# Seven-product up projections of a decoder trunk: combinations of the activations in four pinned portions, sums kept in the other block's buffer, added weight blocks loaded ahead of the down projections

## The chip, the cores and the metric

One core of one Trainium2 chip. The metric is device time in microseconds (us) of one execution of the whole program, which is one launch. The engines are named as the profile names them: PE (TensorE matmul), DVE (VectorE), ACT (ScalarE), POOL (GpSimd) and SP (SyncE, which here only issues transfers). A line such as L94 is line 94 of the kernel.

## The reference

Two layers of a decoder trunk on one sequence of 512 positions with 1024 features, in float32. Per layer:

```python
h = modulate(x, norm_ffn1, sh1, sc1)
x = x + 0.5 * (1 + g1) * swiglu(h, w1, w3, w2)       # FFN 1
h = modulate(x, norm_mix, sh2, sc2)
x = x + (1 + g2) * token_mix(h, ...)                 # gated delta rule and latent attention
h = modulate(x, norm_ffn2, sh3, sc3)
x = x + 0.5 * (1 + g3) * swiglu(h, w1, w3, w2)       # FFN 2

def swiglu(h, w1, w3, w2):
    return (jax.nn.silu(h @ w1) * (h @ w3)) @ w2     # d_ff = 2816
def modulate(x, gain, shift, scale):                 # shift, scale, gate = silu(c) @ ada_w + ada_b
    return rms_norm(x, gain) * (1 + scale) + shift
```

The change touches the FFNs, and the adaLN products that are worked off beside them.

## The kernel before, in words

**Layout and precision.** x and h lie feature-major, [128, 8 k-tiles, 512 positions]. Every product is made in three passes of split operands: a value is the sum of a rounded high part and a low part, and `mm3` adds hi·hi, hi·lo and lo·hi. A weight slab of 512 KB (128x1024) is loaded into a buffer "raw", its high half is a cast on ACT (L121) and its low half a subtraction on DVE (L122).

**One FFN.** d_ff is 22 tiles of 128. The first 4 ("plain"; 6 in layer 0's first FFN, whose first tiles are worked in `begin`) are made by `up`: slabs of w1 and w3, 48 matmuls of 128x512, then a Silu on ACT and a product with the second accumulator on DVE (L514), and a split of the result. The other tiles go two at a time through `pairs`. It makes a 2x2 block product out of seven smaller ones (a Strassen–Winograd form), each 24 matmuls of 128x256. The seven weight forms are, in order, a11, f1, f2, a12, f3, f4 and a22: f1 and f3 are sums of two blocks, made by a load from SP and a second, accumulating load from POOL into the same "L" buffer (`block_sum`, L559); f2 = a11 + f1 (L588) and f4 = a12 + f2 (L591) are made on DVE; each form is then cast (ACT, L581) and gets its low half (DVE, L582). The seven combinations of h are made once per FFN by `fast_acts`, from eight quarters of h in float32, into two buffers "A". The products land in accumulators acc, sc, sm of PSUM; after each product `pairs` copies or adds them (L650 to L672), and Silu and products follow. At step 4 ACT copies the accumulator (L668) and POOL adds the copy (L669).

**The down projection** comes in three parts (`THIRDS`, 8, 8 and 6 tiles of d_ff), worked when 10, 18 and 22 tiles are up, and each adds into x (L407). In the last part, `close` makes the last four of eight tiles in halves, from "spare" slabs whose high and low parts lie in the A buffers and whose raw home is L, and works the next norm in between.

**What sets the order.** Engines run their queues in order. A scheduler sets each queue's order ahead of time, save for what `order` pins. SP issues loads in order and waits at each until its buffer is free: 2 raw, 5 L, 3 each of the split slabs. `self.queue` holds adaLN work: one block is a load of 512 KB into L and one multiply-and-reduce on DVE (L269). `tick(n)` pops n of it, in `up`, after each pair and in the down projections; `drain` pops the rest after the FFN. `rope_tables`, a chain of small DVE and ACT instructions, stands at the end of layer 0's queue.

**The beginning.** `begin` (list `BEGIN`) makes h one k-tile at a time (L1499, ACT's high part L1502, DVE's low part L1467) and adds each to seven slabs' products. The quarters come from POOL, which adds high and low part back together (L462); the first combinations (L471 to L482) are worked right behind it, before the first gate products.

## Time and profile before

| | |
|---|---|
| three runs | 2773.82, 2780.12 (median), 2790.0 us |
| the profiled execution | 2779.66 us |
| its span | 2777.9 us |
| mean granted PE clock | 0.995 |
| busy share PE, DVE, ACT, POOL | 97%, 73%, 47%, 12% |
| HBM read | 376.55 MB |
| chain that ended last, by engine | PE 73%, DVE 15%, DMA 5%, ACT 3%, issue 2%, POOL 2% |

The median of the runs lies 0.46 us above the profiled execution. In a timeline, a row has its start, its duration, engine, line, operation, the tiles by name, shapes and, in brackets, how long the engine stood idle before it and who released it. Rows of several instructions have a count behind x. In the windows the columns are the busy times of PE, PEld (weight loads), DVE, ACT and POOL with their counts, the granted clock, the DMA share and GB/s.

### The profile page before, as it was taken

The page shows a single profiled execution, that of the slowest core. Times are in us where ns is not written, and L with a number is a line of the kernel's source. Part 1 is how long each engine was busy: PE and PEld are TensorE (multiplying, and loading weights), DVE is VectorE, ACT ScalarE, POOL GpSimd, SP SyncE. Part 2 cuts the span into 40 slices and gives each one's busy share as a digit, 9 for nine tenths or more (in the row PEclk, how much of TensorE's full clock was granted, in tenths as well). Part 3 has the DMA queues.
Part 4 walks back from the last instruction along what each step waited for, and adds up shares of the span by engine and source line. Part 5 has one row for each costly group of instructions (what it writes and reads, how often), then busy time and mean ns, then how long its engine had stood idle before and what let it go on. Part 6 is the DMA issues. An engine that isn't in the chain of part 4 may idle for free.

```text
span 2777.9 us, 44536 instructions
## 1 busy us (share of the span) xinstructions
PE 2705.7 (97%) x17168; PEld 2401.9 (86%) x17168; DVE 2023.3 (73%) x3990; ACT 1299.2 (47%) x2540; POOL 335.3 (12%) x433
## 2 busy tenths in 40 slices
PE   7899999999999999999999999999999999999999
PEld 6889897788888888999989898887888888989988
DVE  7778778867668767876678787787767686686755
ACT  3535345454446535534445353554444564353533
POOL 2001004200011011111011010150000011111100
PEclk9999999999999999999999999999999999999999
DMA  7587742322222353777427777332222223456642
GB/s 282 154 246 225 225 159 92 99 66 80 70 78 78 109 186 88 236 231 183 138 69 222 225 227 227 121 104 92 71 85 64 80 78 118 160 142 200 156 132 85
DMA packets 118870, 394.66 MB, mean 142 GB/s; under 512 B 13441, under 2 KB 16129, under 8 KB 118657
## 3 DMA queue, kind: packets, MB, share of 16 engines
q1 hardware_dynamic: 106128, 350.38, 38.2%
q0 software_dynamic: 10080, 36.70, 7.6%
q10 hardware_dynamic: 2448, 4.72, 0.4%
q8 instruction: 135, 2.21, 0.3%
q14 instruction: 79, 0.64, 0.1%
HBM read 376.55 MB, written 15.20 MB: 141 GB/s over the span
## 4 chain that ended last, share of the span: by engine, by line
PE 73%; DVE 15%; DMA 5%; ACT 3%; issue 2%; POOL 2%; SPq 0%; ACTq 0%; POOLq 0%; DVEq 0%
PE acc L94 52%; PE sc L94 14%; PE sm L94 4%; DMA raw<-in_ffn_w 3%; PE sm L99 2%; DVE L L269 2%; DVE wlo L122 2%; PE po L94 1%; DMA L<-in_ffn_w 1%; DVE wlo L582 1%; DVE cv L722 1%; DVE L L854 1%; DVE L L856 1%; DMA raw<-in_w_out 1%; ACT whi L121 0%
## 5 line engine op out<-in xcount | busy, mean ns | idle before, releaser
L94 PE MATMUL acc<-hhi,whi 128*128 128x512 f32 (+1 forms) x1368 | 506.4, 371 | 10.5 <-DVE cv L722 5.7
L121 ACT CAST whi<-raw 128x512 fp32r<-128x512 f32 (+2 forms) x554 | 320.3, 606 | 395.0 <-PE acc L94 305.8
L94 PE MATMUL acc<-hlo,whi 128*128 128x512 f32 (+1 forms) x1368 | 487.2, 356 | 1.8 <-DVE hlo L1467 0.6
L94 PE MATMUL acc<-hhi,wlo 128*128 128x512 f32 (+1 forms) x1368 | 486.7, 356 | 0.0
L94 PE MATMUL acc<-O,whi 128*128 128x512 f32 x1472 | 455.1, 390 | 0.5 <-DVE O L136 0.5
L122 DVE TENSOR_TENSOR wlo<-raw,whi 128x512 fp32r<-128x512 f32 (+2 forms) x554 | 393.8, 729 | 69.4 <-ACT whi L121 62.2
L94 PE MATMUL acc<-A,whi 128*128 128x256 f32 (+1 forms) x1808 | 348.7, 292 | 7.8 <-ACT cv L668 7.8
L94 PEld LDWEIGHTS acc<-O,whi 128*128 128x128 f32 x1472 | 275.0, 188 | 57.8 <-DVE O L136 1.7
L94 PEld LDWEIGHTS acc<-A,whi 128*128 128x128 f32 x1808 | 287.0, 192 | 14.5 <-ACT cv L668 9.4
L94 PEld LDWEIGHTS acc<-hhi,whi 128*128 128x128 f32 x1368 | 259.6, 190 | 41.9 <-issue 8.3
L94 PEld LDWEIGHTS acc<-hhi,wlo 128*128 128x128 f32 x1368 | 259.2, 189 | 38.1 <-DVE wlo L122 0.9
L94 PEld LDWEIGHTS acc<-hlo,whi 128*128 128x128 f32 x1368 | 260.4, 190 | 32.8 <-POOL hlo L392 3.0
L94 PE MATMUL acc<-O,wlo 128*128 128x512 f32 x736 | 286.6, 389 | 0.0
L94 PE MATMUL acc<-A,wlo 128*128 128x256 f32 (+1 forms) x904 | 263.6, 292 | 1.0 <-DVE wlo L582 1.0
L582 DVE TENSOR_TENSOR wlo<-raw,whi 128x1024 fp32r<-128x1024 f32 x140 | 170.6, 1221 | 93.9 <-ACT whi L581 89.3
L581 ACT CAST whi<-raw 128x1024 fp32r<-128x1024 f32 x140 | 146.4, 1046 | 191.9 <-PE acc L94 87.2
L581 ACT CAST whi<-L 128x1024 fp32r<-128x1024 f32 x105 | 109.9, 1047 | 153.8 <-DMA L<-in_ffn_w 37.5
L94 PEld LDWEIGHTS acc<-A,wlo 128*128 128x128 f32 x904 | 173.9, 192 | 3.7 <-DVE wlo L582 1.2
L407 DVE SCALAR_TENSOR_TENSOR M<-acc,gate,M 128x512 f32<-128x512 f32 (+1 forms) x112 | 77.5, 692 | 131.5 <-PE acc L94 124.3
L269 DVE SCALAR_TENSOR_TENSOR L<-L,kph 128x1024 f32<-128x1024 f32 x142 | 171.4, 1235 | 0.0
L94 PEld LDWEIGHTS acc<-O,wlo 128*128 128x128 f32 x736 | 138.2, 188 | 28.7
L559 POOL DMA_DIRECT2D L<-in_ffn_w x70 | 61.2, 875 | 729.7 <-DMA L<-in_ffn_w 257.4
(431 smaller groups left out, 5499.1 us busy)
## 6 DMA issues: line engine op xcount, KB each, us to landing
raw<-in_ffn_w SPq DMA_DIRECT2D x166, 512.0 KB, 4.6
L<-in_ada_w SPq DMA_DIRECT2D x142, 512.0 KB, 4.7
raw<-in_w_in SPq DMA_DIRECT2D x108, 512.0 KB, 3.5
L<-in_ffn_w SPq DMA_DIRECT2D x105, 512.0 KB, 4.8
L<-in_ffn_w POOLq DMA_DIRECT2D x70, 512.0 KB, 7.7
raw<-in_w_branch_a SPq DMA_DIRECT2D x16, 512.0 KB, 3.5
raw<-in_w_branch_b SPq DMA_DIRECT2D x16, 512.0 KB, 3.5
raw<-in_w_out SPq DMA_DIRECT2D x16, 512.0 KB, 3.6
```

Of the source, the lines that this page charges most:

```text
L94: i = self.nc.tensor.matmul(*a, **k)
L99: i = self.nc.tensor.transpose(*a, **k)
L121: nc.scalar.copy(hi[:, s], raw[:, s])
L122: nc.vector.tensor_sub(lo[:, s], raw[:, s], hi[:, s].bitcast(F32))
L269: self.order(self.nc.vector.scalar_tensor_tensor(raw, raw, 1.0, self.condb, ALU.mult, ALU.mult, accum_out=mod[:, o:o + 1]))
L407: self.nc.vector.scalar_tensor_tensor(self.x[:, m, a:b], ps[:, a:b], gate[:, m:m + 1], self.x[:, m, a:b], ALU.mult, ALU.add)
L559: nc.gpsimd.dma_start(t, w13[l, m2, half2].rearrange("p w k c -> p (w k c)"), accum_op=ALU.add)
L581: nc.scalar.copy(hi, t)
L582: nc.vector.tensor_sub(lo, t, hi[:].bitcast(F32))
L722: nc.vector.scalar_tensor_tensor(acc[:, s:], ps[:, :SEQ - s], w[j], acc[:, s:], ALU.mult, ALU.add)
L854: nc.vector.tensor_mul(tv, f[:, j + 1:, j:j + 1].to_broadcast([P, n, w]), x[:, j:j + 1, :w].to_broadcast([P, n, w]))
L856: nc.vector.tensor_sub(x[:, j + 1:, :w], x[:, j + 1:, :w], tv)
```

## The change

Six edits:

1. `begin` writes the quarters itself, by two more ACT instructions per k-tile; the eight POOL adds go.
2. `fast_acts` works in four portions, all of its ACT and DVE instructions pinned. The first two run inside the last two plain tiles, behind the splits of their slabs; the other two in steps 0 and 1 of the first pair.
3. f2 is formed in f1's buffer (L) rather than in a11's (raw).
4. The loads of the next pair are issued in steps 1, 2, 4, 5 and 6 of a pair rather than 2 to 6, and the next pair's forms start at step 2, not 3. `early_sums` issues f1 and f3 of the first pair behind the plain tiles, and of the pair behind a down projection, ahead of that projection.
5. At step 4 DVE adds the accumulator itself (new L670).
6. In the last down projection of an FFN, each tile works off one block (ticks (1, 1) rather than (0, 0)), and the rope tables stand at place 10 of the queue rather than at the end.

```diff
-            for j in range(2):
-                for i in range(4):
-                    hi, lo = (t[:, 2 * i:2 * i + 2, j * 256:(j + 1) * 256].bitcast(F32) for t in (self.hhi, self.hlo))
-                    nc.gpsimd.tensor_add(self.quarter(i, j), hi, lo)
...
+        ordered = self.order
...
-                nc.scalar.copy(hi, t[n])
-                nc.vector.tensor_sub(lo, t[n], hi.bitcast(F32))
+                ordered(nc.scalar.copy(hi, t[n]))
+                ordered(nc.vector.tensor_sub(lo, t[n], hi.bitcast(F32)))
...
         split(places[2], b12)
+        yield
         minus_sum(b11, b21)
...
-        def up(m):
+        def up(m, make):
             s1 = up_slab(w1, m)
             s3 = up_slab(w3, m)
+            next(make)
...
             st["f1"] = block_sum(m + 1, 0, m + 1, 1)
+            if sums_first:
+                st["f3"] = block_sum(m + 1, 0, m, 0)
             yield st
...
-            f2, f4 = st["a11"], st["a12"]
-            nc.vector.tensor_add(f2, f2, st["f1"])
+            f2, f4 = st["f1"], st["a12"]
+            nc.vector.tensor_add(f2, f2, st["a11"])
...
-                    if step in (2, 3, 4, 5, 6):
+                    if step in (1, 2, 4, 5, 6):
                         got = next(nxt, None)
-                        if step == 3 and got is not None:
+                        if step == 2 and got is not None:
                             forms.append(weights(got))
+                    if step in (0, 1):
+                        next(make, None)
...
                         product(x, f, comb[4], False)
-                        u3 = half("cv")
-                        nc.scalar.copy(u3, x)
-                        nc.gpsimd.tensor_add(p5, p5, u3)
+                        nc.vector.tensor_add(p5, p5, x)
...
+        def early_sums(m):
+            lds = loads(m, True)
+            next(lds)
+            return lds
...
-                       (0, 0) if i == 2 else (2, 1))
+                       (1, 1) if i == 2 else (2, 1))
...
-        next(make)
+        lds = early_sums(plain)
         while m < plain:
-            up(m)
+            up(m, make)
             m += 1
-            next(make, None)
-        pairs(range(plain, 10, 2), comb)
+        pairs(range(plain, 10, 2), comb, lds, make)
+        lds = early_sums(10)
         down(0)
-        pairs(range(10, 18, 2), comb)
+        pairs(range(10, 18, 2), comb, lds)
+        lds = early_sums(18)
         down(1)
-        pairs(range(18, FT, 2), comb)
+        pairs(range(18, FT, 2), comb, lds)
...
             ordered(nc.scalar.activation(acts[k][0], h, AF.Identity, bias=sh))
+            for i, (a, b) in enumerate(HALVES):
+                q = self.quarters.get((k // 2, i)) or self.quarter(k // 2, i, 4)
+                ordered(nc.scalar.activation(q[:, k % 2, :], h[:, a:b], AF.Identity, bias=sh))
...
-                self.queue.append(self.rope_tables)
+                self.queue.insert(10, self.rope_tables)
```

The first place is DVE's queue at the end of the beginning, in the kernel before: the last low part (hlo), then combinations of the quarters (c, cv into A), then the low half of a slab and the first gate product.

```order
L1467 SCALAR_TENSOR_TENSOR hlo_127<-g_440,mod_77,hhi_126 128x512
L479 TENSOR_TENSOR c_88_528<-c_88_528,c_92_536 128x512
L476 SCALAR_TENSOR_TENSOR c_89_530<-c_89_530,cv_542 128x512
L472 TENSOR_TENSOR A_544<-c_88_528,A_544 128x512
L472 TENSOR_TENSOR A_544<-c_89_530,A_544 128x512
L476 SCALAR_TENSOR_TENSOR c_88_528<-c_88_528,cv_540 128x512
L476 SCALAR_TENSOR_TENSOR c_89_530<-c_89_530,c_91_534 128x512
L472 TENSOR_TENSOR A_544<-c_88_528,A_544 128x512
L476 SCALAR_TENSOR_TENSOR c_88_528<-c_88_528,c_90_532 128x512
L122 TENSOR_TENSOR wlo_473<-raw_471,whi_472 128x512 x2
L514 TENSOR_TENSOR g_479<-g_479,sc_213 128x512
```

The same place in the changed kernel, whose L511 is the gate product:

```order
L1474 SCALAR_TENSOR_TENSOR hlo_127<-g_462,mod_77,hhi_126 128x512
L122 TENSOR_TENSOR wlo_497<-raw_495,whi_496 128x512 x2
L511 TENSOR_TENSOR g_503<-g_503,sc_223 128x512
L511 TENSOR_TENSOR g_509<-g_509,sc_255 128x512
L511 TENSOR_TENSOR g_515<-g_515,sm_285 128x512
```

The eight rows of combinations stand further back now, behind the slabs of the last two plain tiles.

The second place is SP's queue in a pair between two down projections of layer 0's first FFN. Before, the next pair's loads are f1, f3 and a22 (L), then a11 and a12 (raw), then two adaLN blocks:

```order
L554 DMA L_1866<-in_ffn_w 128x1024
L554 DMA L_1934<-in_ffn_w 128x1024
L554 DMA L_2006<-in_ffn_w 128x1024
L554 DMA raw_1900<-in_ffn_w 128x1024
L554 DMA raw_1968<-in_ffn_w 128x1024
L267 DMA L_2042<-in_ada_w 128x1024
L267 DMA L_2045<-in_ada_w 128x1024
```

In the changed kernel the same pair's loads are these, with a11 first:

```order
L552 DMA raw_1892<-in_ffn_w 128x1024
L552 DMA L_1858<-in_ffn_w 128x1024
L552 DMA L_1957<-in_ffn_w 128x1024
L552 DMA L_2027<-in_ffn_w 128x1024
L267 DMA L_2063<-in_ada_w 128x1024
L552 DMA raw_1989<-in_ffn_w 128x1024
L267 DMA L_2066<-in_ada_w 128x1024
```

a11 stands ahead of the three loads into L, and an adaLN block ahead of a12.

The third place is the end of layer 0's first FFN, its last down projection. On SP before, the four spare slabs (into L) and the first slabs of the stage (raw) stand together:

```order
L118 DMA L_3452<-in_ffn_w 128x768
L118 DMA raw_3329<-in_ffn_w 128x768
L118 DMA L_3458<-in_ffn_w 128x768
L118 DMA raw_3359<-in_ffn_w 128x768
L118 DMA L_3464<-in_ffn_w 128x768
L118 DMA L_3470<-in_ffn_w 128x768
L267 DMA L_3798<-in_ada_w 128x1024
```

In the changed kernel the spare slabs (L_3477 to L_3495) come behind the stage's slabs and the blocks of its ticks (L_3440, L_3474):

```order
L267 DMA L_3440<-in_ada_w 128x1024
L118 DMA raw_3409<-in_ffn_w 128x768
L118 DMA raw_3443<-in_ffn_w 128x768
L118 DMA raw_3501<-in_w_in 128x1024
L267 DMA L_3474<-in_ada_w 128x1024
L118 DMA L_3477<-in_ffn_w 128x768
L1271 DMA spill<-M_63 128x512
L118 DMA L_3483<-in_ffn_w 128x768
L118 DMA raw_3509<-in_w_in 128x1024
L118 DMA raw_3517<-in_w_in 128x1024
L1271 DMA spill<-M_63 128x512
L118 DMA L_3489<-in_ffn_w 128x768
```

On DVE of the changed kernel, the multiply of the last block, the last spare slab's low half and two slabs of the mix stand ahead of the row that empties the first half's accumulator:

```order
L269 SCALAR_TENSOR_TENSOR L_3474,mod_77<-L_3474,kph_64 128x1024
L122 TENSOR_TENSOR A_3341<-L_3495,A_3341 128x512
L122 TENSOR_TENSOR A_3341<-L_3495,A_3341 128x256
L122 TENSOR_TENSOR wlo_3511<-raw_3509,whi_3510 128x512
L122 TENSOR_TENSOR wlo_3519<-raw_3517,whi_3518 128x512 x2
L407 SCALAR_TENSOR_TENSOR M_63<-acc_3525,gate_194_1266,M_63 128x256
```

Before, the row L407 of the first half stood with no multiply and no spare slab close ahead of it.

## The prediction

> **What bounds the kernel now.** I read the page first: the share of each engine, then the chain that ended last.

> ```profile
> PE 2705.7 (97%) x17168; PEld 2401.9 (86%) x17168; DVE 2023.3 (73%) x3990; ACT 1299.2 (47%) x2540; POOL 335.3 (12%) x433
> ```

> TensorE (PE) is busy for 97% of a span of 2777.9 us, and the change leaves its matmuls alone. So a gain can only come out of stretches in which PE waits or runs below its own pace. What I need is a list of those, with the releaser of each. The view of waits, PE alone, gives it (engine and line, who released it, us in total, times, longest).

> ```profile
> PE acc L94 <- ACT cv L668: 7.8, 8, 2.4
> PE sc L94 <- DVE g L514: 7.4, 1, 7.4
> PE sc L94 <- DVE wlo L582: 7.4, 5, 2.8
> ...
> PE acc L94 <- DVE wlo L582: 1.0, 1, 1.0
> ```

> Three rows lie in the seven-product pairs (L668 is the copy at step 4, L582 the low half of a weight form): 7.8 + 7.4 + 1.0 = 16.2 us. One row, L514, is a single wait where the first gate product is made after the kernel's beginning. These four rows bear on the change. Around the single wait, PE's timeline has this:

> ```profile
> 76.07 0.79 PE L94 MATMUL sc<-hhi,whi 128*128 128x512 f32 x1 [7.36 <-DVE g L514]
> ...
> 82.11 0.39 PE L94 MATMUL sc<-hhi,wlo 128*128 128x512 f32 x1
> 82.33 0.39 PE L94 MATMUL sc<-hhi,whi 128*128 128x512 f32 x1
> ...
> 83.95 0.39 PE L94 MATMUL sc<-hlo,whi 128*128 128x512 f32 x1
> ```

> From 82.33 to 83.95 lie seven steps, 0.23 us each. From 76.07 to 82.33, 15 matmuls took 6.26 us instead of 15 x 0.23 = 3.45. So the wait of 7.36 us drew 2.8 us of slow matmuls behind it. The windows show why, in the column behind POOL's busy time, which is the granted clock:

> ```profile
> 68.50:84.60 16.10, 8.74 (x26) 6.80 (x26) 13.17 (x20) 11.31 (x20) 2.40 (x2) 0.68 0.49 125
> ```

> It is 0.68 here. The place is worth 7.4 + 2.8 = 10.2 us.

> **The beginning: -10.2 us.** Who keeps L514 late? VectorE's (DVE) timeline:

> ```profile
> 61.96 0.75 DVE L1467 SCALAR_TENSOR_TENSOR hlo<-g,mod,hhi 128x512 fp32r<-128x512 f32 x1 [0.79 <-ACT hhi L1502]
> 65.35 1.76 DVE L479 TENSOR_TENSOR c<-c,c 128x512 f32<-128x512 f32 x1 [2.64 <-POOL c L462]
> ...
> 73.72 1.28 DVE L122 TENSOR_TENSOR wlo<-raw,whi 128x512 fp32r<-128x512 f32 x2
> 75.33 1.28 DVE L514 TENSOR_TENSOR g<-g,sc 128x512 f32<-128x512 f32 x2 [0.33 <-ACT g L513]
> ```

> Between the last low part (62) and the slab's (73.72) stand eight instructions of the combinations, the first waiting 2.64 us for GpSimd's (POOL) quarter add. ScalarE (ACT) stands in the same queue; it can neither load its table nor make the first Silu before the combinations are split:

> ```profile
> 61.20 0.73 ACT L1502 ACTIVATE hhi<-g,mod 128x512 fp32r<-128x512 f32 x1 [3.22 <-DVE mod L1500]
> ...
> 72.26 1.13 ACT L121 CAST whi<-raw 128x512 fp32r<-128x512 f32 x2
> 73.41 1.28 ACT L513 ACT_TABLE_LOAD   x1
> 74.70 1.57 ACT L513 ACTIVATE g<-acc 128x512 f32<-128x512 f32 x3
> ```

> New on ACT are 16 instructions that write the quarters, two for each of eight k-tiles. The nearest row is an ACT of this shape with a bias, 0.5 us:

> ```profile
> 402.63 0.49 ACT L391 ACTIVATE g<-g,mod 128x256 f32<-128x256 f32 x1
> ```

> In the new order DVE goes from the last low part straight to the slab and the gate products. ACT's chain from 61.9 is then: two quarters of 0.5 each, two casts 1.13, table 1.28, first Silu about 0.6, so 65.9; DVE's product ends about 66.6. PE is busy with the last sums until 76.07 - 7.36 = 68.7, so 2 us of cover remain. The stall and its slow matmuls go. What is late next would be the slab, but its casts at 72.26 wait for no transfer. The combinations move behind the slab splits of the last two plain tiles, two portions of some 5 to 7 DVE rows each, beside 11 us of matmuls per plain tile (48 x 0.23).

> Of the 16 ACTs only the two ahead of the first slab casts delay PE's first matmul (+1.0); the others lie in ACT's idle time (3.22 us in the row at 61.20). Against this stand the eight POOL adds that go, the last of them these:

> ```profile
> 62.79 2.53 POOL L462 TENSOR_TENSOR c<-hhi,hlo 128x512 f32<-128x512 f32 x2 [6.19 <-DVE hlo L1467]
> ```

> They let DVE wait, but PE is the bound of the beginning. I take 0, between -1 and +1.

> **The pairs: -16.2 us, and +6.7 of new waits.** A pair is seven products of 24 matmuls, each like this one on the chain that ended last, so 7 x 2.88 = 20.16 us:

> ```profile
> 205.18 2.88 PE acc L94 x24
> ```

> The waits on L668 come from a late transfer, as SP's queue of issues and ACT's timeline show:

> ```profile
> 236.01 6.76 SPq L554 DMA_DIRECT2D L<-in_ffn_w  x3
> 243.61 2.72 SPq L554 DMA_DIRECT2D raw<-in_ffn_w  x2
> ```

> ```profile
> 250.87 1.05 ACT L581 CAST whi<-raw 128x1024 fp32r<-128x1024 f32 x1 [3.85 <-DMA raw<-in_ffn_w]
> 251.82 0.58 ACT L668 COPY cv<-acc 128x512 f32<-128x512 f32 x1
> ```

> The next pair's first form (a11, into raw) is loaded behind three loads into L, which take SP 6.76 us of issue, and the copy that frees the accumulator stands behind its cast. The change loads a11 ahead of them, since f2 no longer keeps its buffer, and drops L668 and POOL's add (L669): DVE adds from the accumulator itself. Its price is that of the PSUM add next door:

> ```profile
> 233.83 0.68 DVE L672 TENSOR_TENSOR g<-g,sc 128x512 f32<-128x512 f32 x1
> ```

> That is +0.7 us of DVE per pair. DVE has room for it in the fullest pair that I found, 17.27 of 20.30:

> ```profile
> 1585.70:1606.00 20.30, 20.18 (x168) 20.18 (x168) 17.27 (x23) 10.76 (x17) 3.54 (x3) 1.00 0.72 237
> ```

> Behind each down projection the first f1 came late too, and held the chain on DVE:

> ```profile
> 191.09 1.23 DVE L588 TENSOR_TENSOR raw<-raw,L 128x1024 f32<-128x1024 f32 x1 [7.04 <-DMA L<-in_ffn_w]
> ```

> There the sums now are loaded a whole down projection ahead. So all 16.2 us go. What is late next is a loop through one L buffer. f1's buffer is now held until f4's sum, and the next f1 goes into the buffer that the pair's first adaLN block frees. The loop's durations, from the transfers around 205 to 270 and around 1575 to 1640 and from DVE's and ACT's rows there:

> ```profile
> L<-in_ffn_w SPq DMA_DIRECT2D x6, 512.0 KB, 5.3
> ...
> L<-in_ffn_w POOLq DMA_DIRECT2D x4, 512.0 KB, 7.9
> ```
> ```profile
> L<-in_ada_w SPq DMA_DIRECT2D x7, 512.0 KB, 9.2
> raw<-in_ffn_w SPq DMA_DIRECT2D x6, 512.0 KB, 8.1
> L<-in_ffn_w POOLq DMA_DIRECT2D x6, 512.0 KB, 8.3
> L<-in_ffn_w SPq DMA_DIRECT2D x6, 512.0 KB, 5.8
> ```
> ```profile
> 219.49 1.22 DVE L269 SCALAR_TENSOR_TENSOR L<-L,kph 128x1024 f32<-128x1024 f32 x1
> ...
> 222.91 1.22 DVE L582 TENSOR_TENSOR wlo<-L,whi 128x1024 fp32r<-128x1024 f32 x1
> ```

> Load 5.3, accumulating load 7.9, cast 1.05, low part 1.2, f2's sum 1.2, f2's cast 1.05 and low part 1.2, two small DVE rows about 0.9 (L672's 0.68 and one of half its size or less), the adaLN multiply 1.2: 21.0 us against 20.16, so 0.8 late per pair in layer 0, and 21.9 (5.8 and 8.3), 1.7 late, in layer 1. It counts only where two pairs with adaLN work stand in a row after the slack of the early loads is used: the last two of four pairs, and the third behind four plain tiles. Those are 2 pairs in layer 0's first FFN (1.6) and 3 in layer 1's (5.1); the second FFNs have too few adaLN blocks for it. I take 6.7, between 0 and 16.2 (as much as went). Net -9.5.

> [...]

> **Work moved out of the boundaries: -6.1 us.** The rope tables and four adaLN blocks are drained between layer 0's first FFN and its mix. The same 2424 matmuls run in layer 1's window without rope and with two blocks:

> ```profile
> 390.48:767.09 376.61, 369.67 (x2424) 316.20 (x2424) 278.79 (x686) 177.20 (x384) 55.61 (x85) 1.00 0.24 78
> 1765.98:2136.98 371.00, 366.43 (x2424) 314.83 (x2424) 274.70 (x670) 173.57 (x379) 56.81 (x85) 1.00 0.24 79
> ```

> The difference is 5.6 us, and I take all of it (between 3 and 6.5): one drained block instead of four, and the tables go into the first down projection. Layer 1 loses its two drained blocks, 0.5 (0 to 2.4, two of 1.2).

> **Layer 0's last down projection: +2.9 us.** The ticks that now run there put four adaLN loads on SP and in L ahead of the spare slabs. Before, these were issued from this row on, ahead of the stage, and no wait of PE names them:

> ```profile
> 353.15 0.33 SPq L118 DMA_DIRECT2D L<-in_ffn_w  x1
> ```

> Now the fourth spare slab waits for the block of the fourth tick. The stage has four tiles of 18 matmuls (18 x 0.23 = 4.1 us each, 16.5) and then halves of 18 x 0.12 = 2.2 (2.88 / 24 each); the fourth half is due 23 us in. The block's multiply stands about 17 us in, the load takes 5, casts and low parts some 2.5 (1.13 and 1.28 for 1024 columns above), and behind them on DVE stand two more slab rows (1.28) and the L407 that frees an accumulator: near 26. I take +2.9, between 0 and +6. Layer 1's queue is short enough for the spares to come first.

> **The sum.** -10.2 + 0 - 9.5 - 6.1 + 2.9 = -22.9. The profiled execution took 2779.66 us (span 2777.9), the median of the three runs is 2780.12, so I subtract from either: about 2757 us. With the best ends (-11.2, -16.2, -8.9, 0) it is -36.3 and 2743 to 2744; with the poorest (-9.2, 0, -3, +6) -6.2 and 2774.

> **Rivals.** (1) *The f1 loop has slack and the spare slabs come in time.* For it: over the whole run such a load takes less, by the page:

> ```profile
> L<-in_ffn_w SPq DMA_DIRECT2D x105, 512.0 KB, 4.8
> ```

> Against it: the crowded stretches are these pairs. It gives -22.9 - 6.7 - 2.9 = -32.5, 2747. Chance 0.17. [...]

> (2) *The other side: the L buffers become the bound of every pair with adaLN work.* Early sums hold two of five L buffers, f1 a third for longer, and adaLN blocks wait for what is left. For it: raw loads of 8.1 and adaLN loads of 9.2 in the layer 1 window, so a loop with 8.1 instead of 5.8 takes 24.2; against it: loads of L itself stay at 5.8. Over the 22 such pairs (8, 3, 9 and 2 in the four FFNs) the middle, 23.0, costs (23.0 - 20.16) x 22 = 62, less the 6.7 counted: 2757 + 55 = 2812. It makes the kernel slower by 0.5% from (22.9 + 13.9 + 6.7) / 22 = 2.0 us late, a loop of 22.1 in every such pair. Chance 0.05. (3) *The gap at the beginning is half refilled*, by the quarters on ACT or by slab transfers that now queue behind f1 and f3 on SP. Against it: 2 us of cover on ACT. It gives back some 9 of the 10.2 where the wait is again long enough for the clock to fall: 2766. Chance 0.10. (4) *The change doesn't do what it says in the pairs and at the boundary*: the waits only change their name, since the same transfers and the same DVE work stay in the same stretches. It gives -10.2 + 2.9, so 2772. Chance 0.10. My own forecast has the remaining 0.58.

> **How the numbers follow.** The predicted time is 2757, the likeliest case. The range, 2742 to 2772, takes in rival 1, rival 3, nearly all of my own case's bounds and half of rival 4; outside are rival 2 and the tails. About 0.5% (13.9 us) is what a measurement of this kernel can tell from no change. Faster than 2766.2: 0.54 of my 0.58, rival 1's 0.17, half of rival 3 (0.05), a little of rival 4 (0.03), 0.79. Slower than 2794: 0.04. The rest, 0.17, is within.

> **What would show it.** Right: PE has no wait of over 1 us on the first gate product, and the granted clock around 68 to 85 is 1.00; the waits on the step 4 accumulator are gone; PE's waits in the pairs are on the low part of f1 or f2, released by a transfer into L, in the third and fourth pair between down projections and mainly in layer 1; 2 to 4 us of waits late in layer 0's last down projection, behind spare slabs; the mix window of layer 0 is 371 long. Wrong: waits on f1 or f2 in every pair with adaLN work (rival 2), a new PE wait of several us before 85 (rival 3), or a mix window still at 376 (rival 4).

## The result and the profile after

| | before | after |
|---|---|---|
| runs | 2773.82 to 2790.0 us (4) | 2735.41 to 2742.08 us (4) |
| median | 2783.39 us | 2738.93 us |
| profiled execution, span | 2779.66, 2777.9 us | 2742.08, 2740.3 us |

The ratio is 0.9843, with a 95% interval of 0.9809 to 0.9876. Run again beside two experiments, the changed kernel gave 0.9864 (0.9841 to 0.9886). So it is faster by 1.4 to 1.6%; the two intervals together reach from 1.1 to 1.9%. The forecast of 2757 had the sign, but 2738.9 lies below its range (2742 to 2772). Profile against profile the gain is 37.6 us, and the sum had 22.9.

The page's first row after the change, and PE's waits:

```profile
PE 2695.0 (98%) x17168; PEld 2396.7 (87%) x17168; DVE 2006.5 (73%) x4025; ACT 1285.4 (47%) x2519; POOL 266.9 (10%) x390
```
```profile
PE acc L94 <- ACT O L135: 2.2, 1, 2.2
PE acc L94 <- DVE M L407: 2.2, 1, 2.2
...
PE acc L94 <- ACT g L653: 0.5, 2, 0.3
```

The four rows on which the prediction stood (16.2 us in the pairs, 7.4 at the first gate product) are gone. New are 2.2 us on L407, 2.2 us on L135, and 0.5 us in the pairs; the wait of 1.5 us on a slab's cast at 27 us (L1483, now L1490) has grown to 2.3. PE's busy time also fell by 10.7 us, although its instructions are the same 17168: some of the busy time before was slow matmuls (5.96 us of it at a clock of 0.50 from 324.31 to 331.14 us, for one).

**Where the time came from.** Both traces have the same matmuls in the same order but for fewer than a hundred, so the start of the n-th in one less that in the other shows where a gain is made. The beginning and the matmuls right behind it gave 11.1 us, the pairs 22.0, the start of layer 0's mix 6.1. The last down projection of layer 0's first FFN took 3.6 back. That of its second FFN took 4.8, of which 3.2 came back in the plain tiles behind it, where the kernel before had waits on a slab (L121, 1.1 us, and L122, 0.5) and slow matmuls of its own (a clock of 0.50 from 1433.64 to 1437.06 us). The rest, some 3.5, lies in places of at most 1.7.

At the beginning DVE now goes from the last low part (L1474) to the slab and the gate product:

```profile
57.95 0.75 DVE L1474 SCALAR_TENSOR_TENSOR hlo<-g,mod,hhi 128x512 fp32r<-128x512 f32 x1 [0.80 <-ACT hhi L1509]
64.48 1.29 DVE L122 TENSOR_TENSOR wlo<-raw,whi 128x512 fp32r<-128x512 f32 x2 [5.79 <-ACT whi L121]
66.91 1.28 DVE L511 TENSOR_TENSOR g<-g,sc 128x512 f32<-128x512 f32 x2 [1.14 <-ACT g L510]
```

The window behind it is clean, at a granted clock of 1.00 where it was 0.68:

```profile
68.00:85.00 17.00, 17.00 (x77) 14.08 (x76) 16.21 (x24) 10.48 (x19) 2.92 (x2) 1.00 0.43 138
```

The longest pair before was the first behind layer 0's second down projection. Its first matmul, its wait and the first matmul of the next pair are these:

```profile
319.13 0.28 PE L94 MATMUL acc<-hhi,whi 128*128 128x256 f32 x1
...
325.18 0.58 PE L94 MATMUL sc<-A,wlo 128*128 128x256 f32 x1 [2.78 <-DVE wlo L582]
...
344.92 0.28 PE L94 MATMUL acc<-hhi,whi 128*128 128x256 f32 x1
```

The same pair after the change:

```profile
303.62 0.28 PE L94 MATMUL acc<-hhi,whi 128*128 128x256 f32 x1
...
323.78 0.28 PE L94 MATMUL acc<-hhi,whi 128*128 128x256 f32 x1
```

It took 25.79 us with a wait of 2.78, and takes 20.16. The other 2.8 us were slow matmuls: the clock over this pair was 0.87, and it is 1.00 now. I call what a pair takes beyond 20.04 us, first to last matmul, its excess. Over all 35 pairs it was 23.9 us and is 1.9.

In layer 0's last down projection the row that empties the accumulator does stand behind slab rows on DVE, and PE waits for it, with slow matmuls behind (18 in 3.77 us instead of 2.16):

```profile
367.37 1.89 DVE L122 TENSOR_TENSOR wlo<-raw,whi 128x512 fp32r<-128x512 f32 x3
369.17 1.26 DVE L407 SCALAR_TENSOR_TENSOR M<-acc,gate,M 128x256 f32<-128x256 f32 x3
```
```profile
369.80 3.77 PE L94 MATMUL acc<-O,A 128*128 128x256 f32 x18 [2.16 <-DVE M L407]
```

### The profile page after: what moved, and what is told of

Same layout as the page of the kernel before. It is cut to its first block, busy times and chain, and to the rows that moved or that the text cites. A ratio compares the mean times of both kernels' runs of the same rounds, so it can differ in the third digit from the quotient of the medians.

```text
span 2740.3 us, 44511 instructions
## 1 busy us (share of the span) xinstructions
PE 2695.0 (98%) x17168; PEld 2396.7 (87%) x17168; DVE 2006.5 (73%) x4025; ACT 1285.4 (47%) x2519; POOL 266.9 (10%) x390
## 4 chain that ended last, share of the span: by engine, by line
PE 82%; DVE 9%; issue 3%; ACT 3%; POOL 2%; DMA 1%; SPq 0%; ACTq 0%; POOLq 0%; DVEq 0%
PE acc L94 57%; PE sc L94 16%; PE sm L94 5%; PE sm L99 2%; DVE wlo L122 2%; PE po L94 1%; DVE cv L729 1%; DVE L L861 1%; DVE L L863 1%; POOL g L821 0%; ACT whi L121 0%; POOL g L823 0%; POOL O L842 0%; DMA raw<-in_w_in 0%; ACT hhi L389 0%
## 5 line engine op out<-in xcount | busy, mean ns | idle before, releaser
L121 ACT CAST whi<-raw 128x512 fp32r<-128x512 f32 (+2 forms) x554 | 320.0, 607 | 429.2 <-PE acc L94 241.1
L94 PE MATMUL acc<-hhi,whi 128*128 128x512 f32 (+1 forms) x1368 | 506.3, 371 | 11.1 <-DVE cv L729 5.8
L94 PE MATMUL acc<-hlo,whi 128*128 128x512 f32 (+1 forms) x1368 | 487.6, 357 | 1.2 <-POOL hlo L392 0.3
L94 PE MATMUL acc<-hhi,wlo 128*128 128x512 f32 (+1 forms) x1368 | 486.7, 356 | 0.0
L122 DVE TENSOR_TENSOR wlo<-raw,whi 128x512 fp32r<-128x512 f32 (+2 forms) x554 | 387.9, 719 | 107.8 <-ACT whi L121 101.0
L94 PE MATMUL acc<-O,whi 128*128 128x512 f32 x1472 | 456.3, 391 | 2.7 <-ACT O L135 2.2
L94 PE MATMUL acc<-A,whi 128*128 128x256 f32 (+1 forms) x1808 | 346.6, 291 | 0.7 <-ACT g L653 0.5
L94 PEld LDWEIGHTS acc<-O,whi 128*128 128x128 f32 x1472 | 275.9, 188 | 60.4 <-ACT O L135 2.6
L94 PEld LDWEIGHTS acc<-hhi,whi 128*128 128x128 f32 x1368 | 259.5, 190 | 42.4 <-issue 8.3
L94 PEld LDWEIGHTS acc<-hhi,wlo 128*128 128x128 f32 x1368 | 259.4, 190 | 37.3 <-DVE wlo L1491 0.2
L94 PEld LDWEIGHTS acc<-A,whi 128*128 128x128 f32 x1808 | 286.0, 192 | 6.2 <-ACT g L653 0.9
L94 PEld LDWEIGHTS acc<-hlo,whi 128*128 128x128 f32 x1368 | 260.3, 190 | 31.7 <-POOL hlo L392 3.0
L94 PE MATMUL acc<-O,wlo 128*128 128x512 f32 x736 | 287.3, 390 | 0.0
L94 PE MATMUL acc<-A,wlo 128*128 128x256 f32 (+1 forms) x904 | 262.6, 290 | 0.0
L582 ACT CAST whi<-L 128x1024 fp32r<-128x1024 f32 x140 | 147.0, 1050 | 205.0 <-issue 77.0
L583 DVE TENSOR_TENSOR wlo<-L,whi 128x1024 fp32r<-128x1024 f32 x140 | 171.3, 1224 | 35.3 <-ACT whi L582 34.6
L94 PEld LDWEIGHTS acc<-A,wlo 128*128 128x128 f32 x904 | 173.3, 192 | 2.5
L269 DVE SCALAR_TENSOR_TENSOR L<-L,kph 128x1024 f32<-128x1024 f32 x142 | 169.9, 1220 | 5.0 <-DMA L<-in_ada_w 5.0
L583 DVE TENSOR_TENSOR wlo<-raw,whi 128x1024 fp32r<-128x1024 f32 x105 | 128.6, 1224 | 59.1 <-ACT whi L582 58.1
L582 ACT CAST whi<-raw 128x1024 fp32r<-128x1024 f32 x105 | 110.2, 1049 | 118.9 <-PE acc L94 49.3
L94 PEld LDWEIGHTS acc<-O,wlo 128*128 128x128 f32 x736 | 138.5, 188 | 28.9
## 6 DMA issues: line engine op xcount, KB each, us to landing
raw<-in_ffn_w SPq DMA_DIRECT2D x166, 512.0 KB, 4.3
L<-in_ada_w SPq DMA_DIRECT2D x142, 512.0 KB, 5.0
raw<-in_w_in SPq DMA_DIRECT2D x108, 512.0 KB, 3.4
L<-in_ffn_w SPq DMA_DIRECT2D x105, 512.0 KB, 4.5
L<-in_ffn_w POOLq DMA_DIRECT2D x70, 512.0 KB, 8.4
raw<-in_w_branch_a SPq DMA_DIRECT2D x16, 512.0 KB, 3.4
raw<-in_w_branch_b SPq DMA_DIRECT2D x16, 512.0 KB, 3.7
raw<-in_w_out SPq DMA_DIRECT2D x16, 512.0 KB, 3.5
```

Of the source, the lines that this page charges most:

```text
L94: i = self.nc.tensor.matmul(*a, **k)
L121: nc.scalar.copy(hi[:, s], raw[:, s])
L122: nc.vector.tensor_sub(lo[:, s], raw[:, s], hi[:, s].bitcast(F32))
L269: self.order(self.nc.vector.scalar_tensor_tensor(raw, raw, 1.0, self.condb, ALU.mult, ALU.mult, accum_out=mod[:, o:o + 1]))
L582: nc.scalar.copy(hi, t)
L583: nc.vector.tensor_sub(lo, t, hi[:].bitcast(F32))
```

## The experiments

All are the changed kernel with an edit undone or added. Single runs of the kernel before spread from 2769 to 2790 us, so small effects are read from the traces, place by place.

| kernel | time, us | excess of the 35 pairs, us |
|---|---|---|
| before | 2779.66 | 23.9 |
| changed | 2742.08 | 1.9 |
| changed, run again | 2740.51 | 1.2 |
| e1 quarters by POOL | 2743.87 | 4.6 |
| e2 two portions early | 2736.01 | 2.8 |
| e13 both | 2746.78 | 0.6 |
| e3 no early sums | 2740.64 | 2.3 |
| e5 f2 in a11 | 2737.22 | 0.2 |
| e4 copy and POOL's add | 2750.55 | 12.4 |
| e15 = e3 + e5 | 2749.45 | 11.5 |
| e16 = e4 + e5 | 2740.11 | 3.5 |
| e19 = e16 + old steps | 2742.56 | 2.7 |
| e20 = e19 + e3 | 2758.21 | 22.5 |
| e6 no ticks in the last down | 2737.58 | 1.6 |
| e7 rope tables at the end | 2739.60 | 0.6 |
| e8 waits of known size | 2770.34 | not read |

**The beginning: e1, e2, e13.** e1 puts the eight POOL adds back:

```diff
-                ordered(nc.scalar.activation(q[:, k % 2, :], h[:, a:b], AF.Identity, bias=sh))
...
+                    nc.gpsimd.tensor_add(self.quarter(i, j), hi, lo)
```

> The changed kernel with the quarters of layer 0's first FFN made by eight POOL adds again; the combinations stay behind the slabs of the last two plain tiles. Theory (the place of the combinations was the gap): PE has no wait of over 1 us on the first gate product, the matmuls up to the first pair end within 1 us of the changed kernel. Rival (the POOL adds were the gap): a wait of 3 to 7 us there again, and 2 to 3 us of slow matmuls behind it.

The first pair began within 0.3 us of the changed kernel's. e2 calls two portions of `fast_acts` ahead of the first gate products:

```diff
+        make = self.fast_acts(comb)
+        if begun:
+            next(make)
+            next(make)
         m = first_begun() if begun else first()
```

> The changed kernel with ACT's quarters, but the first two portions of the combinations worked ahead of the first gate products, as before. Theory (the place was the gap): a PE wait of 2 to 5 us on the first gate product, and up to 3 us of slow matmuls behind it, so 3 to 8 us lost up to the first pair. Rival (the POOL adds were the gap): no wait of over 1 us.

It lost 0.5 us. Its DVE shows why: the first combination needs no late quarter and starts ahead of the last low part (L1477).

```profile
58.50 0.68 DVE L475 TENSOR_TENSOR c<-c,c 128x512 f32<-128x512 f32 x1
59.37 0.75 DVE L1477 SCALAR_TENSOR_TENSOR hlo<-g,mod,hhi 128x512 fp32r<-128x512 f32 x1 [0.19 <-ACT hhi L1512]
```

So neither theory holds as I put it: each half of the edit removes the gap alone. e13 undoes both (the two diffs above, with one more `next`):

> Both halves of the edit at the beginning undone together: POOL makes the quarters, and two portions of the combinations stand ahead of the first gate products. Theory (the gap needs both, a late last quarter and the combinations in front; each half of the edit alone removes it): PE waits 5 to 8 us on the first gate product and 2 to 3 us of slow matmuls follow, 7 to 11 us lost up to the first pair. Rival (something else of the change, the pinned order or the loads, removed it): under 2 us.

PE waits 8.0 us again and 9.4 us are lost up to the first pair. DVE waits for POOL and then works the combinations:

```profile
PE sc L94 <- DVE g L517: 8.0, 1, 8.0
```
```profile
60.79 0.75 DVE L1484 SCALAR_TENSOR_TENSOR hlo<-g,mod,hhi 128x512 fp32r<-128x512 f32 x1 [0.79 <-ACT hhi L1519]
64.19 1.76 DVE L481 TENSOR_TENSOR c<-c,c 128x512 f32<-128x512 f32 x1 [2.65 <-POOL c L461]
```

**The pairs, one edit undone: e3, e5, e4.** e3 loads f1 and f3 where they were before:

```diff
-            lds = loads(m, True)
-            next(lds)
-            return lds
+            return loads(m)
```

> The changed kernel with f1 and f3 of the first pairs loaded where they were before, behind the plain tiles and the down projections. Theory (a late f1 held the first pair behind each down projection): those first pairs, which take 20.0 us from first to last matmul in the changed kernel, take 21.5 to 25.7 again in five places, 8 to 14 us in all; the wait in layer 0's second last down projection (about 2 us and slow matmuls) goes. Rival (the L buffers are freed in time now anyhow): under 3 us in all.

The rival: 2.3 us in all. e5 forms f2 in a11's buffer:

```diff
-            f2, f4 = st["f1"], st["a12"]
+            f2, f4 = st["a11"], st["a12"]
```

> The changed kernel with f2 formed in a11's raw buffer as before; the add from the accumulator on DVE stays. Theory (a late a11 cost time only because the copy of step 4 stood behind its cast on ACT): the pairs lose no more than 2 us against the changed kernel. Rival (the raw buffer itself was the cause): pairs between down projections take 21 to 23 us again, 5 us or more in all.

The theory: 0.2 us, less than the changed kernel. e4 undoes step 4:

```diff
-                        nc.vector.tensor_add(p5, p5, x)
+                        u3 = half("cv")
+                        nc.scalar.copy(u3, x)
+                        nc.gpsimd.tensor_add(p5, p5, u3)
```

> The changed kernel with step 4 as before: ACT copies the accumulator, POOL adds the copy; a11's buffer is still freed early. Theory (a11's late load ahead of the copy on ACT was the cause of the step 4 waits): PE's waits on that copy stay under 2 us in all. Rival (the copy and POOL's add were the cause): 5 us or more, in the pairs with adaLN blocks.

Neither. PE does not wait on the copy, as the theory had it, but the pairs lose 12.4 us, 6.0 of them in one. POOL, ACT and PE in that pair:

```profile
1226.20 0.86 POOL L557 DMA_DIRECT2D L<-in_ffn_w  x1 [8.88 <-DMA L<-in_ffn_w]
1226.77 1.58 POOL L672 TENSOR_TENSOR cv<-cv,cv 128x512 f32<-128x512 f32 x1
```
```profile
1228.39 0.42 ACT L633 ACTIVATE cv<-cv 128x256 f32<-128x256 f32 x1 [8.11 <-POOL cv L672]
1228.71 1.03 ACT L582 CAST whi<-L 128x1024 fp32r<-128x1024 f32 x1
```
```profile
1229.79 0.80 PE L94 MATMUL sc<-A,whi 128*128 128x256 f32 x2 [2.37 <-ACT whi L582]
```

POOL's accumulating load stood 8.88 us until SP's load had landed, and the add stands behind it in the queue. ACT's Silu stood 8.11 us for the add, f1's cast stands behind the Silu, and PE waited 2.37 us for the cast. The add's worth of 0.7 us on DVE buys POOL's queue out of this chain.

**The pairs, edits undone together: e15, e16, e19, e20.** e15 is e3 and e5:

> No early sums, and f2 formed in a11's buffer; the add from the accumulator stays. Theory (either of the two edits alone brings f1's low part in time: with f2 in f1's buffer DVE must make f1's low part before f2's sum and the adaLN multiplies, with the early load f1 is there long before): the five first pairs behind down projections that were long before are long again, 21.5 us and more, 7 to 14 us in all. Rival (the add from the accumulator and the shifted steps suffice): under 3 us.

11.5 us in all, 6.6 in the five first pairs, three of which take 21.7 us or more: just short of the theory in the places that it named, far from the rival. DVE in e15, then in e3, behind layer 0's first down projection (L583 on L is f1's low part, L589 f2's sum):

```profile
178.06 1.23 DVE L589 TENSOR_TENSOR raw<-raw,L 128x1024 f32<-128x1024 f32 x1 [6.82 <-DMA L<-in_ffn_w]
179.20 0.74 DVE L407 SCALAR_TENSOR_TENSOR M<-acc,gate,M 128x512 f32<-128x512 f32 x1
179.86 1.22 DVE L269 SCALAR_TENSOR_TENSOR L<-L,kph 128x1024 f32<-128x1024 f32 x1
...
182.15 1.22 DVE L583 TENSOR_TENSOR wlo<-L,whi 128x1024 fp32r<-128x1024 f32 x1
```
```profile
180.34 1.23 DVE L583 TENSOR_TENSOR wlo<-L,whi 128x1024 fp32r<-128x1024 f32 x1 [2.41 <-ACT whi L582]
181.60 1.23 DVE L589 TENSOR_TENSOR L<-L,raw 128x1024 f32<-128x1024 f32 x1
```

A sum that is written into f1's buffer cannot come before f1's low part has read it. In a11's buffer it can, and there it and two adaLN multiplies stood ahead of what PE needed. So the move of f2 is also an edit of DVE's order. e16 is e4 and e5:

> The copy and POOL's add at step 4, and f2 formed in a11's buffer; the early sums stay. Theory (the step 4 waits need a late a11 and the copy behind its cast, and f1's loop is tight only where f1's buffer is held for f2 and POOL's queue has the add): PE waits 4 us or more in all on the copy of step 4, in other pairs than the first ones, and no wait on f1. Rival (the shifted steps of the loads alone bring a11 in time): under 1.5 us on the copy.

Between the two: waits on the copy of 2.4 us, and an excess of 3.5. So e4's 12.4 need f2 in f1's buffer as well as the copy and POOL's add. e19 takes the steps back as well:

```diff
-                    if step in (1, 2, 4, 5, 6):
+                    if step in (2, 3, 4, 5, 6):
...
-                        if step == 2 and got is not None:
+                        if step == 3 and got is not None:
```

> The copy and POOL's add at step 4, f2 in a11's buffer, and the next pair's loads in steps 2 to 6 and its forms from step 3, as before; the early sums stay. Theory (the steps of the loads decide how late a11 is, and with it the copy): PE waits 4 to 8 us in all on the copy of step 4, where the kernel with the new steps waited 2.4. Rival (the steps are neutral): 2 to 3 us.

The theory falls: 1.4 us on the copy, an excess of 2.7. This kernel keeps only the early sums of the edits in the pairs. e20 takes them away too:

> As the kernel with the copy, f2 in a11's buffer and the old steps, but without the early sums too: all edits of the pairs undone, the others kept. In that kernel, which kept the early sums, the pairs lost 2.7 us. Theory (the early sums alone carry the gain in the pairs, the step 4 waits included, since a pair that starts late leaves its transfers late for the next): the pairs lose 18 to 25 us, with 5 us or more of waits on the copy. Rival (the kernel before lost time there for another reason, the adaLN queue or the beginning): under 12 us.

The excess is 22.5 us, and 11.3 of waits on the copy are back. PE's waits on the copy in e19, then in e20:

```profile
PE acc L94 <- ACT cv L671: 1.4, 5, 0.5
```
```profile
PE acc L94 <- ACT cv L671: 11.3, 9, 2.2
```

So the early sums alone take some 19.7 of the 22.5 us, and the three other edits alone (e3) leave 2.3: either is enough. The waits on the copy go with the early sums as well; that a late first pair leaves its transfers late for the next ones is the likely way, but was only argued.

**The boundary: e6, e7.** In the changed kernel the last down projection works off one block behind each of its first four tiles; edit 6 also removes the line of `close` that popped blocks for the other four. e6 works off none:

```diff
-                       (1, 1) if i == 2 else (2, 1))
+                       (0, 0) if i == 2 else (2, 1))
```

> The changed kernel with no adaLN block worked off in the last down projections (ticks 0, 0 as before); the tables stay early. Theory: the wait of 2.2 us and its slow matmuls in layer 0's last down projection go (3.6 us back), and the four blocks drained at the boundary cost 0 to 3 us there. Rival (the spare slabs are late anyhow): the wait stays. Time 2739 to 2742 in a run like the changed kernel's profiled one.

The wait goes (3.6 us back), but four blocks are drained at the boundary, PE waits 2.7 us there on a slab's low part, and 50 us into the mix all of the 3.6 is lost again. e7 queues the tables last:

```diff
-                self.queue.insert(10, self.rope_tables)
+                self.queue.append(self.rope_tables)
```

> The changed kernel with the rope tables at the end of the queue again. Theory (the tables, with their table loads on ACT, were most of the 6 us at the boundary of layer 0's first FFN and mix): 3 to 6 us more in the first 70 us of that mix. Rival (the drained adaLN blocks were): under 1.5 us more.

The start of the mix takes 6.0 us more: one wait behind ACT, and a clock of 0.93 in a window that has 1.00 in the changed kernel.

```profile
PE sm L99 <- ACT cv L1282: 3.8, 1, 3.8
```
```profile
372.50:420.00 47.50, 43.17 (x285) 39.09 (x284) 37.24 (x102) 24.26 (x53) 7.99 (x7) 0.93 0.16 57
```

**Slow matmuls behind a wait: e8.** The low part of a22 is made again n times in chosen pairs:

```diff
+                for _ in range(1 + n):
+                    nc.vector.tensor_sub(lo, t, hi[:].bitcast(F32))
```

> The changed kernel with the low part of a22 made 4 to 7 more times (the same values) in nine pairs of the two second FFNs. Each repeat is 1.14 us of DVE against 3.3 us of slack, so PE waits 1.3 (four repeats), 2.4 (five), 3.5 (six) and 4.7 us (seven). The question is the slow matmuls behind a wait, which the sum of the prediction left out. Theory: waits of 2.4 us or more are followed by matmuls at half pace that cost 1.4 to 2.8 us more, waits of 1.3 us are not. [...]

The waits came out other than I had worked out (0.16, 0.16 and 1.60 for four repeats, 1.11 to 1.21 for five, 2.56 and 4.89 for six, 4.30 for seven). Three of them, and the ten microseconds behind each:

```profile
2570.36 0.39 PE L94 MATMUL acc<-A,wlo 128*128 128x256 f32 x1 [1.20 <-DVE wlo L585]
...
2594.40 0.39 PE L94 MATMUL acc<-A,wlo 128*128 128x256 f32 x1 [2.56 <-DVE wlo L585]
...
2621.50 0.39 PE L94 MATMUL acc<-A,wlo 128*128 128x256 f32 x1 [4.30 <-DVE wlo L585]
```
```profile
2570.40:2580.40 10.00, 10.00 (x82) 9.84 (x83) 8.89 (x10) 5.17 (x8) 0.86 (x1) 1.00 0.63 160
2594.40:2604.40 10.00, 10.00 (x70) 10.00 (x71) 7.56 (x9) 4.22 (x7) 0.86 (x1) 0.83 0.61 157
2621.50:2631.50 10.00, 10.00 (x71) 10.00 (x72) 8.05 (x8) 4.57 (x7) 0.89 (x1) 0.83 0.73 186
```

Behind 1.2 us the clock stays at 1.00 and 82 matmuls pass; behind 2.56 and 4.30 it is 0.83, and 70 and 71 pass, 12 fewer, which are worth 1.4 us at 0.12. PE counts as busy for all ten. The three fit the theory, at the low end of its 1.4 to 2.8 us. They do not make it a rule: what came behind the 2.5 us on L407 in the same run is not shown here, and in e16 (last section) 2.13 us on that line drew next to nothing.

**Away with both costs: e17, e18.** e17 is e5 with ticks (2, 2) in the first two down projections and (0, 0) in the last; e18 also issues the first early sums just ahead of the last plain tile.

> The changed kernel once more, as the measure for the two kernels that run beside it: 0.982 to 0.987 of the kernel before.

> The changed kernel with f2 in a11's buffer, and two adaLN blocks worked off behind every tile of the first two down projections and none in the last. Theory: the pairs lose under 0.5 us (they lost 2.0 in the changed kernel), the wait in layer 0's last down projection (3.6 with its slow matmuls) goes and nothing is drained at the boundary, so 3 to 6 us below the changed kernel. Rival (twelve more loads in the first down projections make slabs or early sums late): 0 to 6 us above it.

> The same, with f1 and f3 of the first pair loaded just ahead of the last plain tile, so that they cannot be issued in the last down projection of the FFN before. Theory: the wait in that projection (2.2 us and slow matmuls, 3.6 in all, where a profile shows it) cannot come, so as fast as the kernel without this edit or up to 4 us faster. Rival: f1 comes late for the first pair, 1 to 4 us slower.

The changed kernel had a median of 2739.14 (ratio 0.9864), e17 2737.53 (0.9858; 0.9838 to 0.9877), e18 2738.38 (0.9866; 0.9846 to 0.9886). The traces show e17's wait in the last down projection of layer 0's first FFN gone (3.5 us back) and an excess of 0.5, but a whole kernel's time does not tell the three apart: e17's median is 1.6 us below the changed kernel's, not the 3 to 6 of its theory. e18's new place made its first pairs wait again (excess 3.3): its rival.

## Why the prediction failed, step by step

- **The beginning** (-10.2) was right: 11.1 us, by the mechanism named, wait and slow matmuls. In it is the later start of PE, 0.7 us, which I had put at 1.0 and set against the POOL adds. That either half of the edit would have done it was not seen.
- **The pairs' gain** (-16.2) was mis-sized. I summed waits. The excess that went is 22.0, net of what came new; 23.9 stood there before. Of the 7.7 between, 4.1 are matmuls at half clock, behind the waits of 2.78 and 2.43 us (0.50 from 324.31 to 331.14 and from 1631.62 to 1635.03 us). I had priced such matmuls at the beginning and left them out here. Another 2.2 are a part of each wait that the view does not count: in the rows at 1604 below, the step from one matmul to the next is 0.54 us instead of 0.12, for a wait of 0.26. The other 1.4 were not traced.
- **The pairs' new waits** (+6.7) were the second error, in size. The loop through the L buffer exists, and the time lost lies in pairs that I had named: 0.1 and 0.4 us in the last two of layer 0's four (I had 0.8 each), 0.7 in each of the last two of layer 1's four (I had 1.7). With f2 in a11's buffer (e5) these four pairs lose nothing. The third pair behind layer 1's plain tiles (1.7) lost nothing. That is 1.9 us in all with what is smaller. In layer 1, SP issues f1's loads for the third and the fourth pair here (the first of the three in each row), and ACT copies the accumulator (L653) in the second pair, casts f1 for the third and the fourth, and casts f2 and copies in the fourth:

```profile
1562.75 3.82 SPq L552 DMA_DIRECT2D L<-in_ffn_w  x3
1584.94 3.75 SPq L552 DMA_DIRECT2D L<-in_ffn_w  x3
```
```profile
1561.52 0.58 ACT L653 COPY g<-acc 128x512 f32<-128x512 f32 x1
...
1576.99 1.05 ACT L582 CAST whi<-L 128x1024 fp32r<-128x1024 f32 x1 [3.54 <-DMA L<-in_ffn_w]
...
1597.89 1.05 ACT L582 CAST whi<-L 128x1024 fp32r<-128x1024 f32 x1 [2.91 <-DMA L<-in_ffn_w]
...
1601.75 1.05 ACT L582 CAST whi<-L 128x1024 fp32r<-128x1024 f32 x1 [0.29 <-DVE L L589]
...
1604.17 0.57 ACT L653 COPY g<-acc 128x512 f32<-128x512 f32 x1
```

From issue to issue the loop took 22.2 us, near the 21.9 of the sum and 2.0 more than a pair. But PE did not wait at f1's low part, as I had said: that was ready 3.3 us ahead of its use in the second pair, and still 1.3 in the third and fourth. It waited for the copy L653, which stands on ACT behind f2's cast (late with f2's sum) and one cast more. In the second pair this copy was done at 1562.10 and PE needed it at 1563.3. So 1.2 of the 2.0 us were covered, and the rest reached PE: the third pair lost 0.7. I had all slack used up by then. The next round, from cast to cast, took 20.90, so the fourth pair lost 0.7 again and not 1.7. PE at that copy:

```profile
1604.26 0.28 PE L94 MATMUL sc<-A,wlo 128*128 128x256 f32 x1
1604.80 0.39 PE L94 MATMUL acc<-A,whi 128*128 128x256 f32 x1 [0.26 <-ACT g L653]
```

The two errors, 7.7 us more gained and 4.8 us less lost than I had, are 12.5 of the 14.7 us that the sum missed.

- **Causes in the pairs.** I gave the waits of step 4 to a11's late load and its buffer. e5 and e19 show that neither buffer nor copy need be touched: the early sums do it.
- **The boundary** (-6.1) was right for layer 0: its mix window of 2424 matmuls went from 376.61 to 371.06 us (5.6 forecast), and e7 shows that the tables alone are worth 6.0. The 0.5 forecast for layer 1's boundary did not come; that the start of layer 0's mix gave 6.1 all the same is chance.

```profile
372.85:743.91 371.06, 366.39 (x2424) 314.83 (x2423) 273.54 (x668) 173.68 (x379) 56.93 (x85) 1.00 0.24 79
```

- **The last down projection** of layer 0's first FFN (+2.9) was right in place, row and nearly in size: 3.6 net, of a wait of 2.2 and 1.6 of slow matmuls that the sum had not priced.
- **Not foreseen**: a wait of 2.2 us on L135 in the last down projection of layer 0's second FFN, with its slow matmuls (a clock of 0.50 from 1352.57 to 1355.98 us), behind a slab cast that waited 3.72 us for a transfer.

```profile
1349.17 0.92 ACT L121 CAST whi<-raw 128x512 fp32r<-128x512 f32 x2 [3.72 <-DMA raw<-in_ffn_w]
1350.00 0.61 ACT L135 CAST O<-g 128x512 fp32r<-128x512 f32 x1
```

It is in e5's profile at the same 2.2 us and in e1's at 2.6, is 0.2 in e2's and is missing in e3's; what decides it stays open.

- Of the rivals, the first (slack in the loop, spare slabs in time) came nearest: most of the 6.7 did not come, but the spare slabs did come late. It gave 2747, since it had the short sum of waits.

## What to carry to other kernels

Price a wait of a busy TensorE with what the traces show behind such waits: here those of 2.16, 2.56, 2.78 and 7.36 us drew 1.6, 1.4, 2.8 and 2.8 us of slow matmuls, one of 2.13 us drew next to nothing, and the profile counts slow matmuls as busy (10.00 of the 10.00 us behind the 2.56). Before charging a loop whose period is longer than the work it feeds, find the row at which the engine that counts will stop (here a copy behind the late casts), the lead that the loop has there, and the number of rounds. Where several edits aim at the same wait, undo them in pairs: the early sums and the move of f2, undone one at a time, looked worthless here (2.3 and 0.2 us of excess against 1.9), and undone together they cost 11.5.

## What the runs showed of the hardware

Slow matmuls came behind waits of 2.16 us in the changed kernel (18 matmuls in 3.77 us), 2.56 us in e8 (a clock of 0.83 over the 10 us behind it) and 2.78 us in the kernel before (0.87 over the pair). They did not come each time. The same wait on L407 in e16 was 2.13 us, and the 18 matmuls behind it took 2.39 us, near the 18 x 0.12 = 2.16 of their full pace:

```profile
370.86 2.39 PE L94 MATMUL acc<-O,A 128*128 128x256 f32 x18 [2.13 <-DVE M L407]
```

The wait on L407 left 1.89 us idle in one cell of the changed kernel; in e16 the cells cut it into 1.76 and 0.37. The waits, 2.16 and 2.13 us, are nearly the same, so their length did not tell these two apart; the idle time within a cell did. Here are these cells, of the changed kernel and then of e16, each with its length, PE's busy time and, third from the end, the clock:

```profile
366.11:369.53 3.42, 1.53 (x13) 1.32 (x12) 3.42 (x8) 0.00 (x0) 0.00 (x0) 1.00 0.10 25
369.53:372.94 3.41, 3.14 (x15) 3.17 (x16) 2.09 (x6) 1.20 (x3) 0.00 (x0) 0.50 0.78 281
```
```profile
367.08:370.49 3.41, 1.65 (x14) 1.45 (x13) 3.41 (x8) 0.00 (x0) 0.00 (x0) 1.00 0.11 23
370.49:373.90 3.41, 3.04 (x25) 3.07 (x26) 2.68 (x7) 1.23 (x4) 0.00 (x0) 1.00 0.87 277
```

That the idle time within a cell decides in general was not shown: in the kernel before 1.57 us drew a slow stretch and 1.77 us did not. The changed kernel's profile has three such stretches (mean clock 0.998) and e2's none (1.000), which is one reason why single runs do not rank them.
